# Input stage of a hybrid decoder block: high products first, rows of x between its halves, more of the stage in a written order

## The chip, the cores and the metric

The kernel runs on one core of one Trainium2 chip. The metric is the device time of one execution in microseconds. The profile is one execution taken by the hardware profiler; its times count from the first instruction.

## The reference

One layer of a decoder block on x (1024 positions, 1024 channels, float32), with two token mixers beside each other and a convolutional gated MLP:

```
h = RMSNorm(x)
[z_a | q | k | v | gate logits] = h @ W_in            # 1024 x 5888
y_a = u * (causal 128x128 spatial mix of RMSNorm(v_a)) # u, v_a = split(GELU(z_a))
y_b = dilated sliding-window attention(rope(q), rope(k), v), 3 head groups
merged = sigmoid(g_A) * (y_a @ P_A) + sigmoid(g_B) * (y_b @ P_B)
x = x + merged @ W_out
x = x + (GELU(causal_dwconv3(h2 @ W_gate)) * (h2 @ W_val)) @ W_down,  h2 = RMSNorm(x)
out = RMSNorm(x)
```

The rotary tables are cosines and sines of position times eight frequencies. The norm's scale of a row of x is 1/sqrt(mean square + eps).

## The kernel before

**Arithmetic.** Each float32 operand is split into a rounded high part (ACT copies it to the reduced type) and a low part (DVE or POOL subtracts the high part). A product of two operands is three matmul passes: high x high, high weight x low left, low weight x high left; `PASSES` lists them as (weight part, left part). A large product is one step of a seven-product scheme on 2 x 2 quarters (P1 to P7): a weight pair has seven weight operands (B quarters and their sums) against seven left operands A11, A12, A22, S1 to S4 (x quarters and their sums). P2 adds onto P1's PSUM bank, P4 onto P7's, P3 onto P5's, each after the bank's first result has been taken out.

**Input stage.** W_in is worked in 23 pairs of 256 output columns. Pairs 0 and 1 ("plain", `plain_step`) are multiplied before the norm's scale is known: their left operand is the raw x times the channel gain (`raw_left`, halves h = 0, 1 of 512 positions, eight channel tiles kt), and the scale is applied later. From pair 2 (`FIRST`) on the seven-product form runs (`in_product`, L498), on x scaled in place (`scale_x`, L454, by `bc`, the row scales spread over the partitions by PE in `spread`, L387). For the scales, rows of x are loaded as well (`load_rows`, four tiles of 128 rows for each half), squared and summed by ACT (`square_row`), turned into 1/sqrt by POOL (`root`), and put on a diagonal (`diagonal`: DVE for half 0, ACT for half 1). `x_sum` and the accumulating DMAs `x_sum_dma` form the quarter sums, `in_left` and `parts_of` split the left operands.

**Order.** PE's order is the program's everywhere. In the input stage DVE's and ACT's are too, up to product index `ORDERED` of `in_order`; after that the scheduler orders them. `beginning()` (L1048) writes the first 60 us; then a loop runs the products, calls `in_ahead(i, far, look)` (weight loads `far` products ahead, weight splits `look` ahead) and `meanwhile(i)` for what else belongs at index i. Indices 0 to 6 are pair 2 (P1, P2, P6, P7, P5, P4, P3), 7 to 13 pair 3 (P1, P6, P2, P7, P5, P4, P3).

Work that must come some time later is put in by `after(lag, fn)`: each product calls `tick()` after its sixth and twelfth matmul, and `fn` is written `lag` ticks on. The turns of v (`turn_v`, L618: four PE transposes into one of two `tr` PSUM banks, then ACT out of it, with Gelu for pairs 0 and 1) come that way, then `norm_v` and `spatial`.

**Rotation tables.** `rot_tables` (L2176) returns a chain of 39 steps (small DVE operations that reduce the angles, and ACT's sines at the end), 16 ACT spreads (`wide`) and four turns on PE. `some(n)` writes the next n steps of the chain.

**Queues.** SP issues the loads in program order: weights of pair 0 with the first half of x, its second weight tile, the second half of x, weights of pair 1, rows. `chan` (channel gains) and the positions are issued by ACT.

**Up stage.** `beginning_up` (L1889) writes the start of the W_up products (`up_product`, L1776; blocks ff of 128 gate and 128 value columns) by hand for DVE and ACT. `up_ahead(loads, opened)` splits weight operands up to index `opened` of `order`; where the low part is DVE's it goes on a list, and `low(n)` writes the next n of that list. `first_taps(ff)` writes the first half's convolution.

Of the kernel before, what the change touches and what calls it, by code (L numbers as in the profile page):

```python
# [20 lines left out]
P = 128  # L21
S = 1024
D = 1024
# [70 lines left out]
def block_kernel(  # L94
# [65 lines left out]

    waiting = []
# [105 lines left out]
    def weight_op(st_a, st_v, t3s, key, name, t3_tile, op, sum_eng, lo_eng):  # L267

        if name == "P1":
            src = st_a[:, :QK]  # L270
        elif name == "P2":
            src = st_a[:, QK:]
        elif name == "P6":
# [5 lines left out]
            src = st_a[:, :QK]  # L279
        elif name == "P7":  # L280
            src = t3s.pop(key).rearrange("p (k c) -> p k c", k=QK)
        elif name == "P5":
            src = st_v[:, :QK]
        elif name == "P4":
            b21, t2 = flat(st_a[:, QK:]), flat(st_a[:, :QK])
            sum_eng.tensor_tensor(b21, b21, t2, ALU.subtract)
            src = st_a[:, QK:]
        else:
            src = st_v[:, QK:]
        to_parts(op[:, 0], op[:, 1], src, lo_eng)  # L290

    def in_op(n, name):
        i = counts["in_op"]
        counts["in_op"] += 1
        op = G1[:, 4 + i % OPS_IN, :].rearrange("p (a k c) -> p a k c", a=2, k=QK)
        weight_op(
            raws[n, 0], raws.get((n, 1)), in_t3, n, name,
            lambda: wt.tile([P, HALF], F32, name=f"wt3_{n}", tag="t3", bufs=1),
            op, nc.vector, nc.vector,
        )  # L300
        in_ops[n, name] = op
# [4 lines left out]
    ORDERED = 6  # L306
# [33 lines left out]
    nc.scalar.dma_start(chan, per_channel)  # L340
# [6 lines left out]
    load_x(1, range(KT))  # L347
    in_load(1, 0)
    load_rows(0)
# [148 lines left out]
    def in_product(n, name):  # L498
# [9 lines left out]
        for kt in range(QK):  # L508
            for i, (w, a) in enumerate(PASSES):
                nc.tensor.matmul(  # L510
                    acc, op[:, w, kt, :], left[LEFT[name], kt][:, a, :],
                    start=opened and kt == 0 and i == 0,
                    stop=kt == QK - 1 and i == 2,
                    skip_group_check=not opened,
                )
            if kt % 2 == 1:
                tick()
# [69 lines left out]
    def in_final(n, i, h):  # L587
# [3 lines left out]
        if kind == "zv":  # L591
# [3 lines left out]
            if (i, h) == (1, 0):  # L595
                for b in range(NB):
                    after(5 + 2 * b, lambda b=b: norm_v(b))
                    after(10 + 2 * b, lambda b=b: spatial(b))
# [448 lines left out]

    def beginning():  # L1048
# [3 lines left out]
            tr_tile, ident, positions, YC,  # L1052
# [22 lines left out]

        warm_up(12)
        some(5)
# [7 lines left out]
        weight(0, 1, 1)  # L1085
        plain_final(0, 0, 0)
        product(0, 0, 1)
        for kt in range(KT):
            raw_parts(1, kt)
        product(0, 1, 0)  # L1090
        plain_final(0, 0, 1)
        weight(1, 0, 0)
        weight(1, 1, 0)
        for b in range(4):
            square_row(0, b)
        load_rows(1)
        root(0)
        some(14)
        diagonal(0)
        plain_final(0, 1, 0)  # L1100
        weight(1, 0, 1)
        weight(1, 1, 1)
        product(0, 1, 1, (0,))
        for kt in range(QK):
            plain_step(0, 1, 1, 1, kt)
            if kt == 2:
                bc0 = spread(0)
        for kt in range(KT):
            scale_x(0, kt, bc0)
        plain_final(0, 1, 1)  # L1110
# [3 lines left out]
        parts_of("A11")  # L1114
        product(1, 0, 0)
        diagonal(1)
        bc1 = spread(1)
        for kt in range(QK):
# [3 lines left out]
            if kt % 2 == 1:  # L1122
                x_sum_dma(3, kt // 2)
        plain_final(1, 0, 0)
        product(1, 0, 1)
        plain_final(1, 0, 1)
        parts_of("A12")
        in_ahead(0, 9, 2)
        product(1, 1, 0)
        plain_final(1, 1, 0)  # L1130
# [3 lines left out]
        product(1, 1, 1)  # L1134
        in_ahead(0, 9, 3)
        for kt in range(2, QK):
# [5 lines left out]
        return some, wide, turns  # L1142

    def meanwhile(i):
        if i == 0:
            parts_of("S3")
        elif i == 1:
            parts_of("S1")
        elif i == 2:
            parts_of("A22")  # L1150
        elif i == 3:
            parts_of("S4")
# [5 lines left out]
            for b in range(0, NB, 2):  # L1158
                after(1 + b // 2, lambda b=b: turn_v(1, C[1], b))
                after(5 + b // 2, lambda b=b: turn_v(0, C[0], b))  # L1160
        elif i == ORDERED:
# [3 lines left out]
        elif i == ORDERED + 2:  # L1165
            for fn in turns:
                fn()
# [5 lines left out]
    some, wide, turns = beginning()  # L1173
    for i, (n, name) in enumerate(in_order):
        in_ahead(i, 9, 4 if i else 2)
# [3 lines left out]
        in_product(n, name)  # L1179
# [596 lines left out]
    def up_product(ff, name, beside=None):  # L1776
# [9 lines left out]
        for kt in range(QK):  # L1786
            for i, (w, a) in enumerate(PASSES):
                nc.tensor.matmul(  # L1788
                    acc, op[:, w, kt, :], left[LEFT[name], kt][:, a, :],
                    start=opened and kt == 0 and i == 0,  # L1790
                    stop=kt == QK - 1 and i == 2,
                    skip_group_check=not opened,
                )
            if kt % 2 == 1:
# [94 lines left out]
    def beginning_up():  # L1889
# [82 lines left out]
        up_ahead(18, 17)  # L1972
        low(1)
# [6 lines left out]
        first_taps(3)  # L1980
# [3 lines left out]
        low(1)  # L1984
        up_product(3, "P7")
# [6 lines left out]
        up_product(4, "P2", lambda: up_ahead(27, 25))  # L1992
        low(1)
        up_product(3, "P4", lambda: up_ahead(27, 26))
        low(1)
# [180 lines left out]
def rot_tables(nc, lent, wides, bank, ident, positions, out):  # L2176
# [23 lines left out]
    nc.scalar.dma_start(pos, positions)  # L2200
# [110 lines left out]
```

## Time and profile before

| | |
|---|---|
| median of 3 runs | 1390.81 us (1389.86 to 1391.5) |
| the profiled execution | 1391.06 us |
| its span, mean granted TensorE clock | 1389.1 us, 0.996 |
| PE, DVE, ACT, POOL busy | 98%, 74%, 47%, 21% |
| DMA | 237.01 MB, mean 171 GB/s |

A row of the timeline gives the start, the length of the group, the engine, the line, the operation with its tiles, the count, and in brackets how long the engine stood idle before it and what ended that. A row of the waits gives who waited for whom, the total in us, how often, and the longest. In a row of the windows stand the stretch, its length, the busy us and instructions of PE, PEld, DVE, ACT and POOL, the granted clock as a share of full speed, the busy share of the DMA engines and GB/s. A row of DMA issues ends in the median us from issue to landing. `in_P` are the banks of the seven-product input products, `pl` those of the plain ones, `rs_bc` the spread scales, `vt` the turned v, `rot` the turned tables, `uP` and `up` the banks of the up products, `wr` and `up` also the staged weights, `G` and `R` the split operands.

### The profile page before, as it was taken

The numbers are of one execution on the slowest core, as the hardware profiler recorded it, in microseconds if no ns is written. First come the engines' busy times: TensorE is split into PE (matmuls) and PEld (weight loads), VectorE is DVE, ScalarE is ACT, GpSimd is POOL, SyncE is SP. The second block draws the span as 40 slices with busy tenths as digits, with TensorE's granted clock in tenths as the row PEclk, the third lists the DMA queues.
The fourth block names the chain that finished last, engine by engine and source line by source line (L and its number), as shares of the span: only waits on it lengthen the run. The fifth ranks groups of instructions, "written<-read, shape, count | busy, mean of one in ns | idle before, by whom it ended". The sixth has DMA issues, their size and how long they took to land.

```text
span 1389.1 us, 19247 instructions
## 1 busy us (share of the span) xinstructions
PE 1364.6 (98%) x6434; PEld 1130.7 (81%) x6434; DVE 1030.6 (74%) x1880; ACT 655.1 (47%) x1289; POOL 298.1 (21%) x295
## 2 busy tenths in 40 slices
PE   9889999999999999999999999999999999999997
PEld 7767888888888888888788878888888888888886
DVE  7868677686877987867889887766766667676674
ACT  7583355555544333634646444333433335455443
POOL 0111000000221000120001146655566553000003
PEclk9999999999999999999999999999999999999999
DMA  9424535354435997694843133333323327986563
GB/s 352 89 65 130 167 109 169 115 167 134 130 116 193 329 307 256 216 300 140 287 133 104 39 117 103 106 107 113 107 103 110 122 84 254 385 322 221 196 206 122
DMA packets 143875, 237.01 MB, mean 171 GB/s; under 512 B 13728, under 2 KB 57504, under 8 KB 143776
## 3 DMA queue, kind: packets, MB, share of 16 engines
q1 hardware_dynamic: 141248, 231.53, 49.5%
q0 software_dynamic: 1088, 2.10, 0.9%
q10 hardware_dynamic: 1440, 2.16, 0.4%
q8 instruction: 51, 0.84, 0.2%
q14 instruction: 48, 0.39, 0.1%
HBM read 167.77 MB, written 64.29 MB: 167 GB/s over the span
## 4 chain that ended last, share of the span: by engine, by line
PE 85%; DVE 6%; ACT 3%; issue 2%; POOL 2%; DMA 2%; SPq 0%; POOLq 0%; ACTq 0%; DVEq 0%
PE in_P L510 25%; PE uP L1788 19%; PE dn L2046 13%; PE up L1788 8%; PE pa L1260 5%; PE wo_P L1621 4%; PE pl L571 2%; PE pu L1767 2%; PE pb L1260 1%; PE pu L851 1%; DMA ld<-scr 1%; PE pp L835 1%; DVE G L166 1%; PE pm L660 1%; POOL st L903 1%
## 5 line engine op out<-in xcount | busy, mean ns | idle before, releaser
L510 PE MATMUL in_P<-R,G 128*128 128x512 f32 x1008 | 243.8, 394 | 1.8 <-ACT C L530 1.8
L510 PEld LDWEIGHTS in_P<-R,G 128*128 128x128 f32 x1008 | 185.4, 188 | 38.5 <-ACT C L530 2.2
L2046 PE MATMUL dn<-R 128*128 128x512 f32 x924 | 209.6, 389 | 0.0
L2046 PEld LDWEIGHTS dn<-R 128*128 128x128 f32 x924 | 173.4, 188 | 36.0
L165 ACT ACTIVATE G<-wr 128x512 fp32r<-128x512 f32 x126 | 79.1, 630 | 150.4 <-PE in_P L510 114.4
L165 ACT ACTIVATE R<-up 128x512 fp32r<-128x512 f32 x130 | 78.8, 627 | 125.1 <-DVE up L278 40.9
L510 PE MATMUL in_P<-G,G 128*128 128x512 f32 x504 | 124.1, 397 | 2.3 <-DVE C L537 2.3
L1788 PE MATMUL up<-G,R 128*128 128x512 f32 x504 | 121.4, 391 | 1.7 <-DVE R L166 1.7
L1788 PE MATMUL uP<-G,R 128*128 128x512 f32 x504 | 121.2, 389 | 0.0
L1788 PE MATMUL uP<-R 128*128 128x512 f32 x504 | 121.1, 389 | 0.0
L1788 PEld LDWEIGHTS up<-G,R 128*128 128x128 f32 x504 | 94.5, 188 | 22.7 <-DVE R L166 2.2
L510 PEld LDWEIGHTS in_P<-G,G 128*128 128x128 f32 x504 | 93.7, 190 | 21.1 <-ACT G L405 2.5
L1788 PEld LDWEIGHTS uP<-G,R 128*128 128x128 f32 x504 | 94.5, 188 | 19.8 <-issue 0.2
L1788 PEld LDWEIGHTS uP<-R 128*128 128x128 f32 x504 | 94.6, 188 | 19.6
L166 DVE TENSOR_TENSOR G<-wr,G 128x512 fp32r<-128x512 f32 x126 | 87.9, 699 | 24.2 <-ACT G L165 24.0
L166 POOL TENSOR_TENSOR R<-up,R 128x512 fp32r<-128x512 f32 x55 | 84.0, 1527 | 74.5 <-ACT R L165 74.5
L166 DVE TENSOR_TENSOR R<-up,R 128x512 fp32r<-128x512 f32 x75 | 63.0, 841 | 16.1 <-ACT R L165 15.9
L165 ACT ACTIVATE R<-db 128x512 fp32r<-128x512 f32 x77 | 48.1, 626 | 56.3 <-PE dn L2046 45.3
L166 DVE TENSOR_TENSOR R<-db,R 128x512 fp32r<-128x512 f32 x77 | 53.7, 701 | 25.8 <-ACT R L165 25.7
L1260 PE MATMUL pa<-R,G 128*128 128x512 f32 x288 | 67.9, 389 | 0.0
L1260 PEld LDWEIGHTS pa<-R,G 128*128 128x128 f32 x288 | 54.1, 188 | 11.2
L510 PE MATMUL in_P<-G 128*128 128x512 f32 x252 | 62.2, 393 | 0.0
(279 smaller groups left out, 2396.5 us busy)
## 6 DMA issues: line engine op xcount, KB each, us to landing
wr<-in_w_in_dram SPq DMA_DIRECT2D x45, 512.0 KB, 4.1
up<-in_w_up_dram SPq DMA_DIRECT2D x44, 512.0 KB, 3.5
dA<-gd SPq DMA_DIRECT2D x55, 256.0 KB, 5.1
wd<-in_w_down_dram SPq DMA_DIRECT2D x44, 256.0 KB, 5.5
wT<-wd SPq DMA_DIRECT2D x44, 256.0 KB, 3.7
dS<-gS SPq DMA_DIRECT2D x44, 256.0 KB, 4.2
db<-wT SPq DMA_DIRECT2D x44, 256.0 KB, 4.2
gd<-Y SPq DMA_DIRECT2D x42, 256.0 KB, 2.0
```

The costliest lines, as they stand in the source:

```text
L165: nc.scalar.activation(hi, src, AF.Copy)
L166: fn = lambda: lo_eng.tensor_tensor(lo, src, f32(hi), ALU.subtract)
L510: nc.tensor.matmul(acc, op[:, w, kt, :], left[LEFT[name], kt][:, a, :], start=opened and kt == 0 and i == 0, stop=kt == QK - 1 and i == 2, ...
L571: nc.tensor.matmul(acc, plain_ops[n, k, i][:, w, kt, :], raw_x[h, k * QK + kt][:, a, :], start=k == 0 and kt == 0 and p == 0, stop=k == 1 ...
L660: nc.tensor.matmul(pm[:, o : o + P], v[:, c * P : (c + 1) * P], wspT[:, c * 2 // 3, :], start=True, stop=True,)
L835: nc.tensor.transpose(pp[:, i * P : (i + 1) * P], self.pr[:, h, s * P : (s + 1) * P], ident)
L851: nc.tensor.matmul(pu[:, h * HD : (h + 1) * HD], self.pT[:, i, :], vt[:, h * HD : (h + 1) * HD], start=i % n == 0, stop=i % n == n - 1,)
L1260: nc.tensor.matmul(acc, unit[a][kt // 4][:, kt % 4, :], two(R, 8 * h + kt)[:, b, :], start=n == 0 and i == 0, stop=n == len(kts) - 1 and i ...
L1621: nc.tensor.matmul(acc, left[LEFT[name], kt][:, a, blk * P : (blk + 1) * P], out_ops[s][:, w, :], start=name not in SHARED and kt == 0 and ...
L1767: nc.tensor.matmul(acc, plain_up[which, k][:, w, kt, :], left[f"A{h + 1}{k + 1}", kt][:, a, :], start=n == 0 and i == 0, stop=n == KT - 1 ...
L1788: nc.tensor.matmul(acc, op[:, w, kt, :], left[LEFT[name], kt][:, a, :], start=opened and kt == 0 and i == 0, stop=kt == QK - 1 and i == 2, ...
L2046: nc.tensor.matmul(accs[blk], dops[s][:, 0, a, blk * P : (blk + 1) * P], dops[s][:, 1, w, :], start=SEQ[j] not in CONTINUES and kt == 0 an ...
```

## The change

1. `in_product` and `up_product` run their 12 matmuls as four high x high, then four low weight x high left, then four high weight x low left (`HIGH_FIRST`) instead of the three passes for each channel tile.
2. `chan` is issued after the positions. The four row tiles of half 0 are loaded between the two parts of the second half of x.
3. `beginning()` is rearranged: nine chain steps instead of five at the start; the squares stand between the splits of the second half; evacuations of the plain banks (`plain_final`) stand later; the diagonal before the weights of pair 1; A22's high parts are split early; pair 2's P1 stands before the last half of the plain products.
4. Pair 2 and the start of pair 3 are written operation by operation: high and low parts of S1, P4, A22 and S4 stand apart, at indices 0 to 4; the order written by hand reaches to index 10. The turns of v start three ticks after index 4 instead of one after index 3; `norm_v` and `spatial` come four ticks later.
5. The rotation chain is written at index 7, its sines and spreads at 9, its turns at 11 and 12, into a tile of two banks of its own instead of the `tr` banks.
6. In `beginning_up` the weight operand of (4, P1) is split, low part included, before block 2's first taps; block 3's first taps stand one product later; the split of index 26 moves up.

```diff
+    HIGH_FIRST = [(w, a, kt) for w, a in ((0, 0), (1, 0), (0, 1)) for kt in range(D // P // 2)]
...
+    def in_split(n, name):
...
+        src = weight_src(raws[n, 0], raws.get((n, 1)), in_t3, n, name)
+        in_ops[n, name] = op
+        return (
+            lambda: nc.scalar.activation(op[:, 0], src, AF.Copy),
+            lambda: nc.vector.tensor_tensor(op[:, 1], src, f32(op[:, 0]), ALU.subtract),
         )
...
-    ORDERED = 6
+    ORDERED = 10
...
-    nc.scalar.dma_start(chan, per_channel)
...
-    load_x(1, range(KT))
+    load_x(1, range(QK))
+    load_rows(0)
+    load_x(1, range(QK, KT))
     in_load(1, 0)
-    load_rows(0)
     in_load(1, 1)
...
-        for kt in range(QK):
-            for i, (w, a) in enumerate(PASSES):
-                nc.tensor.matmul(
-                    acc, op[:, w, kt, :], left[LEFT[name], kt][:, a, :],
...
+        for i, (w, a, kt) in enumerate(HIGH_FIRST):
+            nc.tensor.matmul(
+                acc, op[:, w, kt, :], left[LEFT[name], kt][:, a, :],
...
-                    after(5 + 2 * b, lambda b=b: norm_v(b))
-                    after(10 + 2 * b, lambda b=b: spatial(b))
+                    after(9 + 2 * b, lambda b=b: norm_v(b))
+                    after(14 + 2 * b, lambda b=b: spatial(b))
...
+    def rot_bank(name):
+        if not rot_halves:
+            t = ps_x.tile([P, 2, HALF], F32, name=name, tag="sc")
+            rot_halves.extend((t[:, 1], t[:, 0]))
+        return rot_halves.pop()
...
         warm_up(12)
-        some(5)
+        some(9)
...
+        product(0, 0, 1)
+        for kt in range(QK):
+            raw_parts(1, kt)
+        square_row(0, 0)
+        square_row(0, 1)
+        raw_parts(1, 4)
+        raw_parts(1, 5)
+        square_row(0, 2)
+        raw_parts(1, 6)
+        raw_parts(1, 7)
+        square_row(0, 3)
+        load_rows(1)
+        root(0)
         plain_final(0, 0, 0)
...
         product(0, 1, 0)
-        plain_final(0, 0, 1)
+        some(12)
+        diagonal(0)
         weight(1, 0, 0)
         weight(1, 1, 0)
...
+        bc0 = spread(0)
+        product(0, 1, 1, (1,))
         for kt in range(KT):
             scale_x(0, kt, bc0)
...
+        a11 = [in_left("A11", kt, quarter(0, 0, kt)) for kt in range(QK)]
+        splits(a11, (0, 1))
         diagonal(1)
-        bc1 = spread(1)
+        splits(a11, (2, 3))
...
+        for n in range(KT):
+            plain_step(1, 0, 0, n // QK, n % QK)
+            if n == 5:
+                bc1 = spread(1)
...
         in_ahead(0, 9, 2)
+        for hi, _ in a22:
+            hi()
         product(1, 1, 0)
...
-        product(1, 1, 1)
+        plain_final(1, 1, 0)
+        product(1, 1, 1, (0,))
         in_ahead(0, 9, 3)
+        in_sums(FIRST, "P4")
+        in_product(FIRST, "P1")
+        product(1, 1, 1, (1,))
...
     def meanwhile(i):
         if i == 0:
             parts_of("S3")
-        elif i == 1:
-            parts_of("S1")
+            in_ahead(0, 9, 5)
+            late["S1"] = [in_left("S1", kt, Z[:, kt]) for kt in range(QK)]
+            for hi, _ in late["S1"]:
+                hi()
         elif i == 2:
-            parts_of("A22")
+            for _, lo in late["S1"]:
+                lo()
+            late["P4"] = in_split(FIRST, "P4")
+            in_ready["op"] += 1
+            late["P4"][0]()
         elif i == 3:
-            parts_of("S4")
+            late["P4"][1]()
+            for _, lo in a22:
+                lo()
+            late["S4"] = [in_left("S4", kt, quarter(0, 1, kt)) for kt in range(QK)]
+            for hi, _ in late["S4"]:
+                hi()
+        elif i == 4:
+            in_ahead(i, 9, 3)
+            for _, lo in late["S4"]:
+                lo()
             x_stack.close()
...
             for b in range(0, NB, 2):
-                after(1 + b // 2, lambda b=b: turn_v(1, C[1], b))
-                after(5 + b // 2, lambda b=b: turn_v(0, C[0], b))
-        elif i == ORDERED:
+                after(3 + b // 2, lambda b=b: turn_v(1, C[1], b))
+                after(7 + b // 2, lambda b=b: turn_v(0, C[0], b))
+        elif i in (5, 6):
+            in_ahead(i, 9, 4)
+        elif i == 7:
+            some(15)
+        elif i == 9:
             some(99)
             for fn in wide:
                 fn()
-        elif i == ORDERED + 2:
-            for fn in turns:
-                fn()
+        elif i in (11, 12):
+            turns.pop(0)()
+            turns.pop(0)()
...
-        in_ahead(i, 9, 4 if i else 2)
+        in_ahead(i, 9, 4 if i > ORDERED - 4 else 0)
...
-        in_product(n, name)
+        if i:
+            in_product(n, name)
         meanwhile(i)
...
         up_product(2, "P5")
-        up_ahead(18, 17)
-        low(1)
+        up_ahead(20, 18)
+        low(2)
         first_taps(2)
...
         up_product(2, "P3")
         low(1)
-        first_taps(3)
         up_product(3, "P6")
         up_ahead(24, 21)
         up_product(4, "P1")
         low(1)
+        first_taps(3)
         up_product(3, "P7")
...
-        up_product(4, "P2", lambda: up_ahead(27, 25))
-        low(1)
-        up_product(3, "P4", lambda: up_ahead(27, 26))
-        low(1)
+        up_product(4, "P2", lambda: up_ahead(27, 26))
+        low(2)
+        up_product(3, "P4")
         up_product(3, "P3")
...
     nc.scalar.dma_start(pos, positions)
+    late_load()
```

110 lines of the change are left out of this document (50 added, 60 removed).

## The prediction

> **What bounds the kernel now.** I read the page first, then the windows of the first 100 us, PE's waits, and the timeline of each engine there.
>
> ```profile
> PE 1364.6 (98%) x6434; PEld 1130.7 (81%) x6434; DVE 1030.6 (74%) x1880; ACT 655.1 (47%) x1289; POOL 298.1 (21%) x295
> 60.00:76.00 16.00, 12.97 (x60) 10.58 (x61) 13.12 (x22) 13.57 (x25) 1.22 (x1) 1.00 0.34 76
> 76.00:83.00 7.00, 5.72 (x19) 4.26 (x18) 5.96 (x10) 3.49 (x9) 0.00 (x0) 0.52 0.26 87
> 83.00:100.00 17.00, 14.31 (x85) 11.56 (x85) 8.98 (x26) 15.78 (x43) 1.66 (x4) 1.00 0.09 28
> PE in_P L510 <- DVE C L537: 2.3, 1, 2.3
> PE in_P L510 <- ACT C L530: 1.8, 1, 1.8
> PE rs_bc L391 <- ACT C L385: 1.8, 1, 1.8
> PE up L1788 <- DVE R L166: 1.7, 1, 1.7
> ```
>
> PE is busy 98% of the span, so only its idle time can be won. Its four longest waits are named above; three are in the input stage, one at the start of the up stage. In the windows (us, PE, PEld, DVE, ACT, POOL, granted clock, DMA) the clock is 0.52 from 76 to 83 us: PE's 5.72 us there hold work for about 3.0, so 2.7 us are lost to the clock.
>
> ```profile
> 30.34 6.40 PE L571 MATMUL pl<-R,G 128*128 128x512 f32 x27
> 38.49 1.37 PE L391 MATMUL rs_bc<-C,ones 128*128 128x128 f32 x8 [1.75 <-ACT C L385]
> ...
> 56.06 2.88 PE L510 MATMUL in_P<-R,G 128*128 128x512 f32 x12
> 60.71 8.48 PE L510 MATMUL in_P<-R,G 128*128 128x512 f32 x36 [1.76 <-ACT C L530]
> ...
> 72.21 0.60 PE L623 MATMUL vt<-ident,C 128*128 128x128 f32 x4
> 75.14 1.96 PE L510 MATMUL in_P<-G,G 128*128 128x512 f32 x6 [2.33 <-DVE C L537]
> 78.38 1.12 PE L623 MATMUL vt<-ident,C 128*128 128x128 f32 x4 [1.28 <-ACT V L628]
> ...
> 93.27 1.64 PE L510 MATMUL in_P<-R,G 128*128 128x512 f32 x6
> 96.03 1.45 PE L2255 MATMUL rot<-ident,YC 128*128 128x128 f32 x8 [1.13 <-ACT YC L2238]
> 98.90 1.14 PE L2255 MATMUL rot<-ident,YC 128*128 128x128 f32 x8 [1.42 <-ACT YC L2256]
> ```
>
> One matmul of 512 columns takes 0.227 us (the last row below: 209.6 us for 924), so a product of 12 takes 2.72 and half of one 1.36; four transposes take 0.45, eight 0.87. What PE loses is the start of a row less the end of the work before it: 38.49 - (30.34 + 27 x 0.227) = 2.0; 60.71 - 58.78 = 1.9; 75.14 - 72.66 = 2.5; 78.38 - 76.50 = 1.9; 96.03 - 94.63 = 1.4; 98.90 - 96.90 = 2.0. With 0.3 for the slower spread at 38.49 that is 12.0 us, and with the clock 14.7.
>
> **The change part by part.** The profiled time is 1391.06, 1.96 over its span and 0.25 over the median; the sum is made on it.
>
> *The start.* The rows of the first 40 us:
>
> ```profile
> 4.72 0.17 DVE L2193 CAST ones<-ones 128x8 f32<-128x8 int32 x1 [3.62 <-DMA ones<-in_positions_dram]
> 14.14 0.33 SPq L338 DMA_DIRECT2D C<-in_x_dram  x1
> C<-in_x_dram SPq DMA_DIRECT2D x1, 512.0 KB, 6.6
> 24.64 1.06 ACT L366 ACTIVATE YC<-YC 128x1024 f32<-128x1024 f32 x1 [1.39 <-DMA YC<-in_x_dram]
> 16.85 2.55 ACT L448 ACTIVATE R<-X,chan 128x512 fp32r<-128x512 f32 x4
> 17.79 2.73 DVE L449 SCALAR_TENSOR_TENSOR R<-X,chan,R 128x512 fp32r<-128x512 f32 x4
> 21.89 0.22 DVE L2193 CAST ones<-ones 128x128 int32<-128x128 f32 x1
> ...
> 25.43 0.29 DVE L2193 TENSOR_TENSOR ones<-ones 128x128 f32<-128x128 f32 x1
> 28.35 0.88 DVE L383 TENSOR_SCALAR C<-ident,rs_x 128x128 f32<-128x128 f32 x4 [2.63 <-POOL rs_x L374]
> 30.62 5.36 DVE L456 SCALAR_TENSOR_TENSOR X<-X,chan,rs_bc 128x512 f32<-128x512 f32 x8 [0.20 <-PE rs_bc L391]
> ```
>
> The rotation chain costs 3.83/14 = 0.27 us an operation (21.89 to 25.72). Nine instead of five stand ahead of DVE's first split: +1.1, less the 0.44 us by which the positions are issued earlier, +0.65. PE follows DVE here, so it is late by 0.6 too; `chan`, now second, is first read at 5.9, which hides its later issue.
>
> Rows 0 to 3 of x, 2 MB, now go ahead of the last four tiles of its second half. By what SP had issued before, 6.0 MB had landed at 14.14 + 6.6 = 20.7 and 7.0 MB at 24.6. Those four tiles end at 6.25, 6.5, 6.75 and 7.0 MB: 21.7, 22.7, 23.6, 24.6 (before, ACT had them from 16.85 on). The bounds are 20.7 and, were 0.5 MB of the larger row transfers to land first, 26; I take the interpolation. ACT: tiles 4 and 5 to 23.4, a square (1.04) to 24.4, tiles 6 and 7 at 0.64 each to 25.7; DVE's low part of tile 7 ends at 26.4. PE wants tile 4 at 22.65 and gets the last at 26.4: the third plain product ends at 26.9, where it ended at 24.8: **+2.1** with the 0.6.
>
> DVE then has 12 chain operations (3.3) and the diagonal (0.9) to 30.6; the rows' squares ended sooner and no longer decide. PE is free at 29.6 and its spread ends at 30.85 instead of 30.4: **+0.45**. From here PE runs unbroken: 12 + 18 matmuls to 37.6, spread, 6 more, and G, the second product of pair 1, starts at 39.8. The wait of 2.0 (2.3 with the slow spread) at 38.49 goes, since `diagonal(1)` now follows the second rows' squares at once, by about 36, before PE asks at 37.6.
>
> *Pair 2.* P1 is put ahead of the last half of the plain products, so its bank is copied out while PE works: 39.8 + 84 x 0.227 = 58.9 for P2, where it was 60.71. The wait of 1.9 is gone. P2, P6, P7, P5 follow without a gap to 69.8: DVE's splits of S2 end at 61.9, S3 at 64.7, S1 at 69.0 (four at 0.6 each after ACT's), and high-first wants a low left part only 8 x 0.227 = 1.8 us into a product. P7's result is added at 69.7, before P4 starts; the wait of 2.5 goes.
>
> What is late next? DVE's queue is unbroken here, and holds the four low parts of A22 (70.4 to 72.8), then P5's addition (73.4); ACT's queue has P5's Gelu behind that, and P3's weight split behind the Gelu (74.0 to 74.6). So P4 loses **0.4** on A22, and P3 starts at 74.6 instead of 72.9: **+1.7**. The wait at 60.71 and this one have changed places.
>
> ```profile
> 74.91 2.49 DVE L406 SCALAR_TENSOR_TENSOR G<-X,G 128x512 fp32r<-128x512 f32 x4
> 77.49 1.57 ACT L628 ACTIVATE V<-vt,rs_x 128x256 f32<-128x256 f32 x4 [2.23 <-DVE G L406]
> 80.68 0.63 ACT L165 ACTIVATE G<-wr 128x512 fp32r<-128x512 f32 x1 [1.11 <-DVE wr L278]
> ```
>
> Then the turns of v. S4's low parts (2.49) end at 77.7, P4's addition at 78.3, its Gelu 79.0, pair 3's P1 split 79.6 and its low part 80.2, three sums of 0.72 to 82.4 (the 80.68 row waits for their like), P6's split 83.0; only then the Gelus that empty the first of the two transpose banks (1.57 for four, 0.8 for two), at 83.8. The third turn now falls at the end of P3, since pair 2's own first turn shares that tick, and needs that bank: PE stands from 78.5 to about 83.7: **+5.2**. This takes the place of the 1.9 at 78.38. After it PE works through pair 3 with no wait I can find.
>
> *The rotation tables.* The chain's end, sines and 16 spreads follow a product earlier than the turns, on two banks of their own; ACT is through at about 102.7 where PE asks at 102.1: of 1.4 + 2.0, **0.6** stays. The v norms and the mixing come four ticks (5.4 us) later; their last stands at tick 28 after P3, the attention buffers open at tick 32, so these 5.4 us cover it, and a loss there could not exceed the same 5.4.
>
> *The clock.* The 0.52 row follows idle times of 2.5 and 1.9 us; one of 5.2 should bring it at least as surely, so I put 2.7 in again. [...]
>
> Input stage: before 14.7; after 2.1 + 0.45 + 0.4 + 1.7 + 5.2 + 0.6 + 2.7 = 13.15. **-1.5 us.**
>
> *The up stage, and high-first everywhere.*
>
> ```profile
> 814.36 0.61 PE L1788 MATMUL up<-G,R 128*128 128x512 f32 x2
> 816.71 2.57 PE L1788 MATMUL up<-G,R 128*128 128x512 f32 x10 [1.74 <-DVE R L166]
> 815.98 0.68 DVE L166 TENSOR_TENSOR R<-up,R 128x512 fp32r<-128x512 f32 x1
> L2046 PE MATMUL dn<-R 128*128 128x512 f32 x924 | 209.6, 389 | 0.0
> ```
>
> Two matmuls into (4, P1) PE waits for its low weights, split at 815.98 behind the taps of block 2. The change splits them before those taps, about 5 us earlier, and high-first asks for them two matmuls later: 816.71 - 814.36 - 0.45 = **-1.9**. If the weight tile lands late, DVE and ACT are held there, but the products behind have 2 to 3 us of slack, which hides it; the cost without that is at most the same 1.9.
>
> The other 290 reordered products neither wait now nor will: their spacing stays if a new stationary operand costs nothing. The down products change it at each matmul and take 0.227 like the rest, so 0; a bound above is in the third rival.
>
> Sum: -1.5 - 1.9 = -3.4: 1391.06 - 3.4 = 1387.7 for the profiled run, **1387.4** as a median.
>
> **The rivals.** 1, *the bank wait is short.* If DVE and ACT reach the Gelus about 3 us sooner than I add up (they idle 1.3 us twice in my chain, for P3's and P1's splits), PE stands 2 us instead of 5.2: **1384.2** with the clock halved as before, 1381.5 with it whole. Against it: DVE's queue is full from 26 us on. 2, *the late tiles of x cost more.* DVE has no gap behind them, so each us is paid at 83.7 again. If the 7.0 MB land at 27, +2.4: **1389.8**; it decides from 0.6 us on, where the gain falls below what can be measured. 3, *high-first costs on PE* (the slower one): the old order uses each high weight twice running, the new one never. If a matmul with a new stationary operand takes 5 ns more, 3528 of them cost 17.6: **1405**; it decides from 1.8 ns on (3.4 + 2.8 over 3528). The down row is against it. 4, *the change does not do what it says in the up stage*, the wait only moving to another split: 1389.3.
>
> **How the numbers follow.** A measurement of this kernel tells about 0.2%, 2.8 us, from no change. Forecast 0.50, rival 1 0.22, rivals 2 and 4 0.18, rival 3 with any other loss of the orders now written by hand 0.10. Faster by over 0.2% (under 1388.0): 0.36 of the forecast and 0.22 of rival 1, 0.58. Slower: rival 3, half of 2 and a tail of the forecast, 0.22. Between: 0.20. The range runs from rival 1 with the clock whole, 1381.5, to 1392.5, rival 2 with the bound of 26 for tile 4 (+4.3 on the forecast) and 0.8 over.
>
> **What would show it.** Right: no wait at `rs_bc` L391 for ACT L385, none of P2 for L530, none at the up product for L166; a `vt` row at about 84 waiting for ACT L628 with some 5 us, and a clock near 0.5 behind it; the pl row of the third product ending near 27. Wrong: a `vt` wait under 2 us; low parts of x's second half after 27; a spacing in the reordered products over 0.229; or a new wait in the up stage.

## The result and the profile after

The changed kernel takes 1393.12 us (median of 20 runs, 1390.69 to 1396.89) where the kernel before takes 1391.59 (20 runs beside them, 1389.07 to 1393.82): a ratio of 1.0014, 95% interval 1.0007 to 1.0021. That is 1.0 to 2.9 us slower, about within the 0.2% (2.8 us) that the prediction called no change, where 3.4 us faster was forecast; the time lies above the stated range of 1381.5 to 1392.5 us. The profiled executions are 1394.24 and 1391.06 us, spans 1392.5 and 1389.1. So the spans of the profiled pair show +3.4, somewhat more than the medians (+1.5).

The longest waits of PE in the changed kernel behind its warm-up (total us, times, longest):

```profile
PE vt L636 <- ACT V L641: 5.1, 1, 5.1
PE rot L2316 <- ACT YC L2317: 3.4, 2, 2.7
PE pl L584 <- DVE R L463: 2.0, 4, 1.2
PE uP L1849 <- DVE Y L1870: 1.6, 1, 1.6
PE in_P L523 <- DVE C L550: 1.2, 3, 0.6
PE in_P L523 <- ACT G L307: 1.2, 1, 1.2
PE uP L1849 <- DVE Y L1881: 0.5, 1, 0.5
```

None of the four waits shown of before is left: `rs_bc` for the diagonal, P2 for its bank, P4 for the addition into C, the up product for the low weights of (4, P1). Others stand there instead. In PE's timeline:

```profile
26.25 2.91 PE L584 MATMUL pl<-G 128*128 128x512 f32 x12
29.00 1.14 PE L405 MATMUL rs_bc<-C,ones 128*128 128x128 f32 x8
36.83 1.05 PE L405 MATMUL rs_bc<-C,ones 128*128 128x128 f32 x8
...
73.09 1.66 PE L523 MATMUL in_P<-G 128*128 128x512 f32 x6 [1.16 <-ACT G L307]
...
76.57 0.60 PE L636 MATMUL vt<-ident,C 128*128 128x128 f32 x4
82.25 1.11 PE L636 MATMUL vt<-ident,C 128*128 128x128 f32 x4 [5.08 <-ACT V L641]
83.02 2.91 PE L523 MATMUL in_P<-R,G 128*128 128x512 f32 x6
...
102.84 0.60 PE L2316 MATMUL rot<-ident,YC 128*128 128x128 f32 x4
106.17 0.66 PE L2316 MATMUL rot<-ident,YC 128*128 128x128 f32 x4 [2.73 <-ACT YC L2317]
107.01 4.61 PE L523 MATMUL in_P<-G,G 128*128 128x512 f32 x12 [0.19 <-DVE C L550]
```

P2 of pair 2 starts at 58.16 us (60.71 before), its P4 at 69.04 (75.14): 6.1 us are won by then. The third turn of v stands for 5.1 us and, with the half clock behind it, takes nearly all of it back; the turns of the rotation tables add 3.6 us of idle time. Two of the rows are too long for their work: six matmuls in 2.9 us at 83.02, and twelve in 4.6 at 107.01. The windows (us, PE, PEld, DVE, ACT, POOL, granted clock, DMA share, GB/s) say why:

```profile
80.34:87.17 6.83, 4.92 (x17) 4.23 (x18) 3.78 (x8) 4.59 (x10) 0.07 (x1) 0.50 0.25 76
107.65:111.06 3.41, 3.41 (x10) 2.67 (x9) 1.75 (x3) 2.99 (x7) 2.43 (x6) 0.50 0.35 135
```

The first stretch at half the clock begins within the idle time that ends at 82.25, the second 1.5 us behind the one that ends at 106.17; before had one such stretch in this stage (76.2 to 83.1). When the mixing of v is done, the first product behind it starts at 151.36 instead of 148.99: the input stage lost 2.4 us. From there to the up stage the changed kernel regains 0.6 (first up product 758.83 against 757.07). The up stage adds 1.7:

```profile
816.13 2.88 PE L1849 MATMUL up<-G,R 128*128 128x512 f32 x12
...
842.38 3.04 PE L1849 MATMUL uP<-opx,R 128*128 128x512 f32 x12 [0.54 <-DVE Y L1881]
845.25 2.93 PE L1849 MATMUL up<-G,R 128*128 128x512 f32 x12
849.83 3.02 PE L1849 MATMUL uP<-G,R 128*128 128x512 f32 x12 [1.65 <-DVE Y L1870]
```

(4, P1), the product P1 of block 4, at 816.13, runs without its wait of 1.7, but PE waits again at 842.38 and 849.83. The stretch from the start of (4, P1) to the thirteenth product behind it takes 39.27 us (816.13 to 855.40) where it took 37.58 (814.36 to 851.94). From there both kernels run alike to the end.

**How far one profile can be trusted.** The changed kernel and the five variants of it below that differ only in the up stage run the same instructions up to there. From the first product behind the mixing (151.36 here) to the first of the up stage (758.83) their profiles take 606.2 to 608.3 us. One profile can therefore be off by 1 us either way, so places are compared within one stretch, and totals by medians.

### The profile page after: what moved, and what is told of

It is laid out like the page before. It is cut to its first block, busy times and chain, and to the rows that moved or that the text cites. A ratio compares the mean times of both kernels' runs of the same rounds, so it can differ in the third digit from the quotient of the medians.

```text
span 1392.5 us, 19210 instructions
## 1 busy us (share of the span) xinstructions
PE 1367.2 (98%) x6434; PEld 1131.8 (81%) x6434; DVE 1032.1 (74%) x1880; ACT 653.9 (47%) x1289; POOL 297.6 (21%) x295
## 4 chain that ended last, share of the span: by engine, by line
PE 83%; DVE 6%; issue 3%; ACT 3%; DMA 2%; POOL 1%; SPq 0%; POOLq 0%; DVEq 0%; ACTq 0%
PE in_P L523 26%; PE uP L1849 18%; PE dn L2106 13%; PE up L1849 7%; PE pa L1322 5%; PE wo_P L1683 4%; PE pu L864 2%; PE pu L1829 2%; PE pb L1322 2%; DMA X<-in_xt_dram 1%; PE pp L848 1%; PE sc L809 1%; PE sc L810 1%; PE pm L673 1%; POOL fm_f L2227 1%
```

## Experiments

The theory after the result, called A below: the input stage's gain is real, but is taken back by two places where ACT is late (at the turns of v and at the tables), with the clock behind them; and the up stage's new order loses more than the wait that it removes. The rivals: high-first costs time at each matmul or makes the new waits; or the waits only move elsewhere when one is removed. Ratios are to the kernel before, run on the same chip; the changed kernel's is 1.0014. A difference to the changed kernel is the difference of the two ratios times 1391 us, and is known to some 1.7 us, less well for the runs of experiment 6.

**1. Only high-first.** The kernel before with this edit, in both product functions:

```
-        for kt in range(QK):
-            for i, (w, a) in enumerate(PASSES):
+        for i, (w, a, kt) in enumerate(HIGH_FIRST):
```

> The kernel before with nothing changed but the order of the matmuls within a product of pair or up stage: high weights first. Theory A (the order costs TensorE nothing, a matmul of 512 columns stays at 227 ns): within 0.5 us of the kernel before, perhaps 0.5 to 1 us faster where a product waits for low parts. Rival (each change of the stationary operand costs): slower by 3528 times the extra of a matmul, 3.5 us for each ns.

Measured: 1391.46 us, ratio 1.0008 (0.9997 to 1.0019); the time alone leaves it open. The groups of the up stage (matmuls; busy us, mean ns) decide, before, changed and this kernel in this order:

```profile
L1788 PE MATMUL uP<-R 128*128 128x512 f32 x504 | 121.1, 389 | 0.0
```
```profile
L1849 PE MATMUL uP<-R 128*128 128x512 f32 x504 | 121.1, 389 | 0.0
```
```profile
L1787 PE MATMUL uP<-R 128*128 128x512 f32 x504 | 121.1, 389 | 0.0
```

The order of the passes costs nothing: a nanosecond a matmul would be 0.5 us in each of these groups. The 116 products from 851.94 us to 1169.05 take 317.11 us in before, and the same 317.11 in the changed kernel (855.40 to 1172.51). The third rival of the prediction is out. This kernel's profile lost time at a stretch of half clock from 62.25 to 65.66 us which the kernel before did not have there, with the same wait ahead of it (below, on the clock), and its stretch of 6.8 us at half lies at 96.39 to 103.22 instead of 76.2 to 83.1.

**2. The turns of v.** The split of pair 3's P6 one product later, so that ACT does not wait for its sums ahead of the Gelus:

```
         elif i in (5, 6):
-            in_ahead(i, 9, 4)
+            in_ahead(i, 9, i - 2)
```

> The changed kernel with one weight split, that of pair 3's P6, asked for one product later, so that ScalarE has the Gelus of the first turned block of v ahead of it. Theory A (PE's 5.1 us at the third turn of v are the wait of ScalarE for the three sums of that split on VectorE): the wait falls to about 1.5 us, the clock stays whole or is halved for a shorter time (up to 2.5 us), so 3.5 to 6 us earlier at pair 3, and 3 to 6 us faster than the changed kernel. Rival 1 (the wait moves on: pair 3's own products then wait for the split): the earlier gain is given back within the next two products, time as the changed kernel. Rival 2 (the mixing and the buffers behind it set the time of the attention's start whatever PE does here): pair 3 starts earlier, but the products after 110 us do not.

Measured: 1388.66 us, ratio 0.9988 (0.9979 to 0.9997), 3.6 us below the changed kernel. ACT in the changed kernel, where P6's split waits for the sums ahead of the Gelus:

```profile
80.84 0.63 ACT L307 ACTIVATE G<-wr 128x512 fp32r<-128x512 f32 x1 [2.89 <-DVE wr L277]
81.38 1.55 ACT L641 ACTIVATE V<-vt,rs_x 128x256 f32<-128x256 f32 x4
```

PE and ACT in this kernel:

```profile
78.58 0.66 PE L636 MATMUL vt<-ident,C 128*128 128x128 f32 x4 [1.57 <-ACT V L641]
```
```profile
77.18 0.61 ACT L307 ACTIVATE G<-wr 128x512 fp32r<-128x512 f32 x1
77.70 1.55 ACT L641 ACTIVATE V<-vt,rs_x 128x256 f32<-128x256 f32 x4
```

The Gelus now follow P1's split at 77.70, where they started at 81.38. The wait is 1.57 instead of 5.08 and the clock stays whole there, 1.00 from 76 to 98 us (the half clock at the tables is left, 0.81 from 98 to 107). The first rival is out; the second is too, as the 4.9 us won at the mixing are still there at 300 us.

**3. The rotation tables.** First each turn in a transpose bank of its own (`rot_bank` replaced by `tr_tile`):

> The changed kernel with each turn of the rotation tables in a transpose bank of its own instead of in one half of a two-bank tile. Theory A (the second turn of a pair waits for ScalarE's copy of the first because both lie in one tile, and the idle time brings the second stretch at half the clock): the waits of 2.7 and 0.7 us at the second and fourth turn fall to 0.5 us or less in all, the clock near 108 us stays whole (1.7 us), so 3.5 to 5 us faster than the changed kernel. Rival (the turns wait for ScalarE's spreads, which are late whatever the bank): the wait stays, only its releaser is another line, and the time is within 0.5 us of the changed kernel.

Measured: 1392.56 us, ratio 1.0018 (1.0007 to 1.0029): no gain. The wait at the turn went, and came back one instruction later, with its half clock (0.72 from 105 to 111 us):

```profile
102.19 1.41 PE L2316 MATMUL rot<-ident,YC 128*128 128x128 f32 x8
106.37 4.62 PE L523 MATMUL in_P<-G,G 128*128 128x512 f32 x12 [2.78 <-DVE C L550]
```

The rival has the time, but neither has the place. The bank does hold up the second turn, but behind it stood another waiter on the same late ACT. The changed kernel's ACT shows the lateness:

```profile
97.55 0.84 ACT L195 ACTIVATE junk_v<-V 128x768 bf16<-128x768 f32 x1
...
99.71 1.28 ACT L2293 ACT_TABLE_LOAD   x1
...
101.84 3.28 ACT L2299 ACTIVATE YC<-ones 128x128 f32<-128x128 f32 x16
105.02 0.61 ACT L307 ACTIVATE G<-wr 128x512 fp32r<-128x512 f32 x1
105.54 0.57 ACT L2317 ACTIVATE YC<-rot 128x512 f32<-128x512 f32 x1
```

The 16 spreads end at 105.0; only then comes a weight split whose low part is next on DVE, ahead of P7's addition (L550), which must empty the bank before P4 writes to it. DVE in the changed kernel:

```profile
105.67 0.69 DVE L308 TENSOR_TENSOR G<-wr,G 128x512 fp32r<-128x512 f32 x1 [2.29 <-ACT G L307]
106.28 0.68 DVE L550 TENSOR_TENSOR C<-C,in_P 128x512 f32<-128x512 f32 x1
```

So the banks and that split were parted together:

```
-        in_ahead(i, 9, 4 if i > ORDERED - 4 else 0)
+        in_ahead(i, 9, 3 if i == ORDERED else 4 if i > ORDERED - 4 else 0)
```

> The changed kernel with each turn of the rotation tables in a transpose bank of its own, and with no weight split asked for ahead of pair 3's P7, so that VectorE's addition of P7 no longer stands behind ScalarE's split, and that behind the 16 spreads. Theory C (the idle time at the tables is ScalarE's lateness, 105.0 us for a split asked for at 102, and it passes from the bank of the turns to the addition of P7 when the banks are parted, 2.8 us in that run): both waits fall, to 0.6 us or less in all, no half clock follows near 107 us (1.7 us), and the time is 4 to 5 us below the changed kernel. Rival (the wait moves once more, to P5's or P4's low weights, whose split is late by the same spreads): 2 to 3 us of idle time appear between 105 and 112 us, and the time is 0 to 1.5 us below.

Measured: 1387.89 us, ratio 0.9975 (0.9965 to 0.9986), 5.4 us below the changed kernel:

```profile
102.34 1.04 PE L2316 MATMUL rot<-ident,YC 128*128 128x128 f32 x8
103.13 2.98 PE L523 MATMUL in_P<-G,G 128*128 128x512 f32 x12
105.95 1.03 PE L2316 MATMUL rot<-ident,YC 128*128 128x128 f32 x8
```

No wait and no half clock here (1.00 from 98 to 115 us): P4 takes 2.8 us to the next row instead of 4.5. The rival is out. The spreads are still late (they end at 104.1, and PE is at the turns from 102.3 on); what counted was who stood behind them.

**4. The rows of x.** Loaded behind the second half again, their squares behind its splits:

> The changed kernel with the rows of x loaded behind the second half of x again, and their squares behind its splits. Theory A (the rows between the halves cost about 1.4 us at the third plain product and win more at the spread of the row scales): the third product ends at 24.8 instead of 26.3 us, the squares end near 29 us, PE waits 2 to 3 us at the first spread, and the second pair starts 0.5 to 1.5 us later than in the changed kernel, which the bank wait at the turns of v hides, since VectorE and ScalarE are then 0.5 to 1 us later as well: 0.5 to 1.5 us slower. Rival (the late tiles are paid at every later point, as VectorE's queue has no gap): 1 to 2 us faster than the changed kernel, the third turn of v included.

Measured: 1393.49 us, ratio 1.0013 (1.0002 to 1.0024): the same as the changed kernel. Both expectations missed:

```profile
24.78 2.88 PE L583 MATMUL pl<-G 128*128 128x512 f32 x12
28.16 1.16 PE L404 MATMUL rs_bc<-C,ones 128*128 128x128 f32 x8 [0.49 <-DVE C L396]
```

The third plain product ends 1.5 us earlier (24.78 against 26.25) and the first spread waits 0.5: 0.8 us earlier in all (28.16 against 29.00). DVE starts to scale x 0.8 earlier too (29.80 against 30.64), but at 38.02 it waits 0.45 for ACT's split of pair 1's weights, which comes no sooner, and from 39.23 (39.52) on it is 0.3 ahead. These 0.3 arrive at the third turn of v, at 81.97 against 82.25, with a wait of the same length (5.10 and 5.08). So most of what the start gains is lost on DVE behind ACT; the rest is passed on, as the rival had it.

**5. The up stage.** Its old beginning in the changed kernel:

> The changed kernel with the beginning of the up stage in its old order of splits and taps; the input stage and the high-first products stay. Theory A (the rewritten order of the up stage loses more to new waits between 826 and 851 us, 3.2 us, than the 1.9 us wait that it removes): the new waits go and the old one of about 1.9 us at the start of (4, P1) comes back, so 1.3 to 2 us faster than the changed kernel. Theory B (high-first itself makes those waits, since a product then asks for its low weights later but all at once): the waits stay in about the same size, 0 to 1 us slower than the changed kernel.

Measured: 1391.50 us, ratio 1.0004 (0.9994 to 1.0013), 1.4 us below the changed kernel. The wait at (4, P1) is back (1.19 at 818.86) and the two later ones are gone; the stretch takes 37.22 us against 39.27. So the rewritten order costs 2 us there, and high-first by itself gains 0.2 to 0.4 (37.58 before, 37.36 in experiment 1's kernel). Next, single steps of the new order, each in the changed kernel: (a) the first taps of block 3 in their old place, ahead of (3, P6).

> The changed kernel with the first taps of block 3 back in their old place, ahead of (3, P6), the early split of (4, P1) and all else as changed. Theory D (these taps, 2.6 us later than before, make the multiplications of P4 and P3 on GpSimd late by 4 us; VectorE waits for them with P7's addition behind, which PE needs): the waits of 0.7 and 1.8 us after 838 us go, and the 1.9 us at (4, P1) stay gone: 2.5 to 3.3 us below the changed kernel. Rival (the lots of low parts at (4, P2), taken two at a time, are what makes VectorE late): the waits after 838 us stay, and the time is within 0.7 us of the changed kernel.

Measured: 1393.73 us, ratio 1.0015 (1.0005 to 1.0025), no gain, stretch 39.10 us. The theory failed: the later wait shrank, and a new one stands before it, at (4, P2), which waits for ACT's copy of P1 out of the same bank:

```profile
824.83 3.03 PE L1849 MATMUL up<-G,R 128*128 128x512 f32 x12 [1.73 <-ACT t L1862]
...
848.25 3.02 PE L1849 MATMUL uP<-G,R 128*128 128x512 f32 x12 [1.25 <-DVE Y L1870]
```

(b) In addition (4, P1) is split ahead of (3, P6), whose sums ACT must wait for:

> The changed kernel with the first taps of block 3 in their old place and, at the start of the up stage's third block, the weights of (4, P1) split ahead of those of (3, P6), which must wait for VectorE's sums. Theory E (the early split of (4, P1) costs VectorE 1.9 us, 1.2 of them idle because ScalarE has that split behind one that waits for VectorE itself; VectorE has no slack from there to 850 us, so it is paid as a wait later, whichever step is moved): VectorE's 1.2 us of idle time ahead of this low part go, the wait of 1.7 us at (4, P2) falls to 0.5 or less, the one of 1.3 us near 848 us to 0.3 or less, and the up stage takes 1.2 to 2 us less than the kernel before's: 2.5 to 3.5 us below the changed kernel. Rival (ScalarE's copy of P1 and GpSimd's multiplications are late for reasons of their own, not by this split): the waits stay within 0.5 us of 1.7 and 1.3.

Measured: 1391.57 us, ratio 1.0008 (0.9999 to 1.0017), stretch 38.05 us. Half right: the wait at (4, P2) fell to 0.24, but the other, 1.25 in (a), grew to 1.65. (c) In addition the splits at (4, P2) one by one again (the changed kernel writes two low parts there at once, a lot of two):

> The changed kernel with the up stage's beginning as before except for one step: the weights of (4, P1) are split ahead of those of (3, P6) and before the first taps of block 2 (the splits at (4, P2) are one there and one behind P4's taps again). Theory F (the wait of 1.65 us near 848 us, which stayed when ScalarE's order was mended, comes from the second of the two lots at (4, P2): it stands on VectorE ahead of P4's taps and makes them, GpSimd's multiplications and the sums behind them about 1 to 2 us late, where the kernel before had 0.7 us to spare): that wait falls to 0.4 us or less, the one at (4, P1) stays gone, and the up stage takes 1.3 to 1.9 us less than the kernel before's, 3 to 3.6 below the changed kernel. Rival (the sums of block 3 are put ahead of P7's addition by the planner whatever these lots do): the wait stays at 1.2 us or more, and the up stage takes as long as the kernel before's within 0.5 us.

Measured: 1390.67 us, ratio 0.9997 (0.9987 to 1.0007), stretch 37.38 us. The wait fell to 1.02, between the two expectations; the stretch, equal to before's, is the rival's. GpSimd's timeline showed a low part between its two multiplications of block 3:

```profile
839.57 1.30 POOL L1879 TENSOR_TENSOR Y<-Y 128x512 f32<-128x512 f32 x1 [3.58 <-ACT Y L1781]
840.82 1.31 POOL L169 TENSOR_TENSOR R<-up,R 128x512 fp32r<-128x512 f32 x1
842.09 1.31 POOL L1883 TENSOR_TENSOR Y<-Y 128x512 f32<-128x512 f32 x1
```

(d) That low part behind them:

> The kernel with the mended lots at (4, P2), and with the low part behind P4's taps left until after P3: on GpSimd a low part of 1.31 us then no longer stands between the two multiplications of block 3 (839.57 and 842.09 us in that run), on VectorE one of 0.68 us no longer stands ahead of P3's addition; every other instruction stays where it is. Theory G (VectorE's sums of block 3 wait for GpSimd's second multiplication, P7's addition stands behind them, and the wait of 1.0 us near 848 us is this low part): the wait falls to 0.3 us or less and the up stage takes 1.0 to 1.5 us less than the kernel before's, 0.8 to 1.3 us below the neighbour. Rival (P7's addition is late for another reason): the wait stays near 1.0 us.

Measured: 1392.41 us, ratio 1.0008 (0.9996 to 1.0019), stretch 37.77 us, the wait 0.90. The rival holds. GpSimd's second multiplication is 1.0 us earlier, counted from the start of (4, P1) (24.7 us behind it instead of 25.7), and now VectorE waits for the next thing that GpSimd does, the sum for block 5's weights, with P7's addition (L1871) still behind:

```profile
844.05 0.69 DVE L276 TENSOR_TENSOR up<-up,up 128x512 f32<-128x512 f32 x1 [1.18 <-POOL t L275]
844.78 1.83 DVE L277 TENSOR_TENSOR up<-up 128x512 f32<-128x512 f32 x1
846.54 0.68 DVE L1871 TENSOR_TENSOR Y<-Y,uP 128x512 f32<-128x512 f32 x1
```

P7's addition starts so many us behind the start of (4, P1): 30.75 before, 32.98 in the changed kernel, 30.92 with the old beginning, 32.79 in (a), 31.74 in (b), 31.06 in (c), 31.47 in (d). None is below before's. The 1.7 us at (4, P1) can be removed, but PE then arrives earlier at a bank that DVE and GpSimd do not empty sooner. That these two engines together set the length of this stretch fits all rows; it was not shown by taking work off them. The planner's place for block 5's sums, ahead of P7's addition, was not moved either.

**6. Together.** The mends of 2 and 3 with (a):

> The changed kernel with four mends at once: pair 3's P6 split asked for one product later, the turns of the tables in banks of their own, no split ahead of pair 3's P7, and the first taps of block 3 in their old place. If each is worth what its own run shows or is expected to show (3.6, 4 to 5 with the parted banks, 2.5 to 3.3 us) and none hides behind another: 10 to 12 us below the changed kernel, 1381 to 1384 us, and 8 to 10 below the kernel before. If the mixing of v sets the time of what follows the third pair: the gains stop at 110 us and the time is 1385 to 1388 us.

Measured: 1383.87 us, ratio 0.9939 (0.9924 to 0.9955). It is 10.4 us below the changed kernel, in the range of the first expectation, but not by its terms: (a) was worth nothing, and the two mends of the input stage make 3.6 + 5.4 = 9.0 by their own runs. The gains do not stop at the mixing. What was left at P3 (1.2 us in the changed kernel, 1.3 here) is ACT's P3 split behind P5's Gelu, so that split was asked for one product earlier (`in_ahead(i, 9, 4)` at the end of index 3), with the old beginning of the up stage, with (b), with (c) and with (d):

> The changed kernel with the three mends of the input stage (P6's split of pair 3 one product later, the turns of the tables in banks of their own, no split ahead of pair 3's P7), with P3's weight split of pair 2 asked for one product earlier, and with the up stage's beginning in its old order. If the wait of 1.3 us at P3 is worth its length now that the wait at the turns of v is short: 1.0 to 1.5 us earlier at pair 3 than without it; with the old order of the up stage 1.7 us less there: 1380.5 to 1382.5 us. If the turns of v only wait that much longer: 1382 to 1383.5 us.

> The same four mends of the input stage, with the up stage's order in which (4, P1) is split ahead of (3, P6) and the first taps of block 3 stand in their old place. By theory E 0.8 to 1.6 us below its neighbour with the old order: 1379.5 to 1381.5 us. By its rival 1.5 to 2 us above that neighbour.

> The same up stage with the four mends of the input stage (P6's split of pair 3 one product later, the turns of the tables in banks of their own, no split ahead of pair 3's P7, P3's split of pair 2 one product earlier). By theory F 1 to 1.5 us below the version with the old order of the up stage, 1380.2 us: 1378.7 to 1379.3 us. By its rival 1380 to 1381 us.

> The same with the four mends of the input stage. By theory G 1379.2 to 1379.7 us, 0.8 to 1.3 us below its neighbour at 1380.5; by its rival 1380 to 1381 us.

Measured: 1380.17 us, ratio 0.9917 (0.9904 to 0.9931); 1380.45, 0.9921 (0.9907 to 0.9934); 1380.49, 0.9923 (0.9911 to 0.9936); 1379.53, 0.9919 (0.9904 to 0.9934). All four beat both kernels, by some 11 and 13 us, and cannot be told apart: as in 5, the up stage's orders (b) to (d) are worth no more than the old one, where theories E and F expected about 1 us less. The last time lies in theory G's range, but not by its mechanism: the stretch from (4, P1) takes 37.09 us in the first of the four and 38.01, 37.30 and 37.78 in the others, so the old order is the shortest, and in the last the wait near its end is still 0.92. The earlier split at P3 is worth its wait: from P2 of pair 2 to pair 3 the first of the four takes 19.7 us (58.57 to 78.25), the kernel of the mends alone 21.1 (57.89 to 79.01). In the first of the four the clock is whole in a window where before has 6.8 us at half:

```profile
60.00:115.00 55.00, 52.62 (x280) 42.57 (x279) 45.89 (x90) 43.18 (x98) 10.38 (x22) 1.00 0.34 89
```

## Why the prediction was wrong

**What held.** *Pair 2*: P2 starts at 58.16 (58.9 said), without the wait for the bank; the wait of P4 is gone, that of P3 has come (1.2 us; 1.7 said). *The diagonal* no longer holds up the second spread. *The turns of v*: 5.1 us of idle time at the third turn for ACT's Gelu, 5.2 said, at 82.25 (83.7 said; PE came to it 1.5 us earlier as well, so that the length fits while both ends were put too late); experiment 2 shows that the place given for it, the split behind three sums, is the cause. *The clock* behind it: 6.8 us at 0.50, as in before. *High-first*: 0. The first and second rival did not come, the third is out.

**Terms off in size.** The third plain product loses 1.5 us, not 2.1; the first spread and A22's low parts lose nothing (0.45 and 0.4 said). These make 1.5 us in the changed kernel's favour, but experiment 4 shows that of 0.8 us won at the start only 0.3 reach the turns of v.

**Step that failed: the rotation tables.** "On two banks of their own; ACT is through at about 102.7 where PE asks at 102.1: of 1.4 + 2.0, 0.6 stays." PE asked at 102.84, ACT was through at 105.0. Two things were missed. ACT had four squares of the v norms (L195, 1.0 us each with its read, between 92.8 and 98.5) and a table load of 1.28 ahead of the spreads. These squares come in the program at index 11 and later, behind the spreads of index 9: the written order binds only the written instructions among each other, and the planner fills the gaps with later work. And I followed only the turns, not what else waits for ACT there: a split, its low part, and P7's addition behind that on DVE. The two banks are one tile, and its second half waits for the copy of its first; with two tiles the idle time was still there. The idle time is 2.73 + 0.69 + 0.19 = 3.6 us; by the prediction's own measure, start less the end of the work before, the loss is 2.9 + 0.4 + 0.8 = 4.1 (106.17 - 103.29, 107.01 - 106.62, 112.75 - 111.91) instead of 0.6: 3.5 off.

**Step that failed: the clock.** I put 2.7 in again, for one stretch of half clock. Behind the idle time at the tables stood a second one of 3.41 us, which cost the twelve matmuls at 107.01 1.7 us. Experiment 3, with banks and split parted, removed wait and stretch together. The row of 0.52 was also misread: the clock fell at 76.2, ahead of the idle time of 1.9 us that ends at 78.38, so the row does not show that 1.9 us bring half clock; whether they prolonged it was not shown. And the loss there was 2.3 us, not 2.7: from 78.38 to 84.27 stand 12 matmuls and 8 transposes, work for 3.6. Rival 1 and the lower end of the range, 1381.5, take the clock as whole behind 2 us of idle time at the turns; no run shows that term. What the runs showed is a whole clock behind 1.57 us there (experiment 2) and behind 1.76 us ahead of P2 in before, and half clock behind 1.78 us ahead of P2 with only high-first.

**Step that failed: the up stage.** "-1.9", with slack of 2 to 3 us behind it. The wait at (4, P1) went as said, but the stretch became 1.7 us longer: 3.6 us off. The fourth rival, that the wait only moves to another split, had the right kind; the wait moved to other steps, of DVE and GpSimd, and grew. I took the slack from products that did not wait, without adding up what the moved steps (1.2 us of idle time and 0.7 of work on DVE ahead of the taps; two lots at (4, P2)) do to the chain that empties the banks.

**The sum.** -3.4 was said. The steps that failed add 3.5 + 1.7 + 3.6, the clock loss of before, put 0.4 too high, adds 0.4, the terms off in size take off 1.5, P3 and the first clock stretch (1.3 and 2.3 us) 0.8, and between 151 and 757 us the execution gained 0.6: +2.9. The spans of the profiled pair show +3.4; the other 0.5 us I have not attributed. The medians show +1.5.

## What to carry to other kernels

When a change writes an order by hand, list for each engine that arrives late everybody who waits for it, not only the first: the parted banks, (a) and (d) each mended one wait and brought up the next. A stretch that PE runs without waits has no known slack until the chain that frees its banks is added up on the other engines. And a gain on PE counts only as far as the engines that end its next long wait share it: of the 0.8 us that the rows' old place won at the start, DVE and ACT brought 0.3 to the turns of v.

## What the runs showed of the hardware

**The clock.** The prediction put half clock down to idle times of 2.5 and 1.9 us. In the traces of the input stage it came in stretches of 3.41 or 6.83 us, and the same wait ahead of P2 (1.8 us) brought one in the kernel with only high-first but none before:

```profile
62.25:65.66 3.41, 3.41 (x10) 2.64 (x9) 2.85 (x5) 3.36 (x6) 0.01 (x1) 0.50 0.89 154
```

In the changed kernel the clock changes at 80.34, 87.17, 107.65 and 111.06 us, which is 6.83, 20.48 and 3.41 us apart, 2, 6 and 1 times 3.41. In the two kernels with the same instructions up to there, the changed one and (a) of experiment 5, the same idle time of 5.08 us at the third turn of v was followed by half clock until 87.17 (6.83 us in all) in one and until 85.58 (3.41 us) in the other, and the work from that turn to the second group of eight transposes took 6.5 us (82.25 to 88.71) and 5.4 (82.81 to 88.23). So behind the same idle time the same work differed by 1 us here, and with only high-first the stretch from the start of P2 to that of P5 took 1.6 us more than in before (9.9 and 8.3).

No limit of the idle time can be read from these traces: 1.94 us ahead of P2 were followed by half clock with only high-first, while in before the clock stayed whole behind 1.9 us ahead of P2 and behind the 2.0 us ahead of the spread at 38.49 (1.00 from 20 to 76 us). By the profile's own column these idle times are 1.78, 1.76 and 1.75 us. What decided between them was not shown.

**DVE beside GpSimd.** In the changed kernel the sum at 845.10 on DVE takes 1.77 us where its like takes 0.68:

```profile
845.10 1.77 DVE L1808 TENSOR_TENSOR own<-Y 128x512 f32<-128x512 f32 x1 [2.17 <-POOL Y L1882]
```

GpSimd has an operation of 1.29 us from 845.03 on, and the sum ends 0.55 us behind it; the other rows of one such operation that take 1.2 us or more from 828 us on lie beside one too. Not each operation beside one is longer: the addition at 849.11 takes 0.67 with one of 1.28 on GpSimd from 849.26 on. What makes the difference was not shown.
